# Cross-entropy loss on one core: a smoother taper of the fourteen loads, and twelve unread products ahead of the last ones

## The chip, the cores and the metric

The kernel runs on one core of one Trainium2 chip. The metric is device time in microseconds (us); a median over several runs is quoted, with the lowest and highest. The profile comes from one profiled execution, and its span (first to last instruction) is some 1.8 us shorter than the device time.

## The reference, cut to what matters

```python
def reference(logits, labels):            # logits [256, 32000] float32, labels [256] int32
    log_probs = logits - np.max(logits, axis=-1, keepdims=True)
    log_probs = log_probs - np.log(np.sum(np.exp(log_probs), axis=-1, keepdims=True))
    return np.array([-log_probs[i, labels[i]] for i in range(batch)])
```

The kernel leaves the maximum out: the loss of a row is log(sum of exp(x) times exp(-x at the label)). All 32.77 MB of logits must be read once.

## The kernel before

Two rows of the logits lie on each of 128 partitions, 64,000 columns in all, loaded in fourteen pieces. ScalarE takes the exp of each piece in place and accumulates its row sum. At the end VectorE adds the partial sums of the second row, TensorE multiplies them into a diagonal matrix that holds exp(-x at the label), a second product adds the sum of the last piece, ScalarE takes the log and one small transfer writes the result.

```python
CHUNKS = [
    14848, 12288, 8832, 6528, 4992, 3776, 2752,
    2368, 1856, 1344, 1344, 1152, 1024, 896,
]
...
        for i in range(2, len(CHUNKS) - 1):
            exps(i)
            if seen[0] == n_of[0] and i == HEAD - 1:
                ...                                   # row 0: reduce, product, log
        nc.vector.reduce_sum(out=sums[:, 1:2], in_=parts[1][:, :], axis=mybir.AxisListType.X)
        nc.tensor.matmul(lane[1][:, :], sums[:, 1:2], diag[1][:, :], start=True, stop=False)
        exps(len(CHUNKS) - 1)
        nc.tensor.matmul(lane[1][:, :], s_last[:, :], diag[1][:, :], start=False, stop=True)
        log_row(1)
        nc.sync.dma_start(...)                        # the 256 results
```

In what follows, "sums product" is the first of the two products at the end and "last product" the second. Each is float32 and appears as two passes of TensorE, a pair. A product whose passes run at TensorE's slow clock is called cold here, at its fast clock warm.

The softmax here doesn't subtract the row's maximum and nothing guards it: scores larger than these inputs give would overflow.

## Time and profile before

| | before |
|---|---|
| device time, median of 3 | 85.26 us (85.17 to 85.44) |
| span of the profiled run, whose device time was 85.8 | 84.0 us |
| bytes read, share of the load queue | 32.77 MB, 92.2% |
| ScalarE busy | 58.9 us, 70% |
| TensorE busy | 1.8 us |

The queue is busy nearly all the time, so the place to look is what comes after the last load has landed. The prediction shows the lines.

### The profile page before, as it was taken

To read this page: it belongs to the slowest core of one execution; us is meant where nothing else is said; L and a number is where in the kernel's file an instruction comes from. 1 tells how busy PE (TensorE), PEld (TensorE's weight loads), DVE (VectorE), ACT (ScalarE), POOL (GpSimd) and SP (SyncE) were. 2 spreads that over 40 slices of the span, in tenths; PEclk is the share of its full clock that TensorE was granted. 3 is DMA by queue.
4 is the path that set the end of the run, shared out by engine and by line. 5 is a ranking of instruction groups with operands and counts; after the bars stand their busy time and mean duration, and the time that the engine had idled before them with its cause. 6 is when DMAs were issued, how large, how long until landed. Compare 5 with 4: busy or idle time off the path is not lost.

```text
span 84.0 us, 126 instructions
## 1 busy us (share of the span) xinstructions
PE 1.8 (2%) x6; PEld 0.3 (0%) x6; DVE 0.8 (1%) x4; ACT 58.9 (70%) x34; POOL 3.0 (4%) x10
## 2 busy tenths in 40 slices
PE   0000000000000000000000002000000000000050
PEld 0000000000000000000000000000000000000000
DVE  0000000000000000000000200000000000000000
ACT  6000000001999998089999999999999999999960
POOL 3000000000072000000000000000000000000000
DMA  9787899998999989979989999999999999999300
GB/s 424 311 368 339 368 453 453 453 453 375 515 491 421 398 374 421 454 320 521 454 370 407 448 448 403 443 428 417 396 422 418 425 412 420 414 413 405 149 0 0
DMA packets 2226, 32.77 MB, mean 390 GB/s; under 512 B 433, under 2 KB 434, under 8 KB 1202
## 3 DMA queue, kind: packets, MB, share of 16 engines
q1 hardware_dynamic: 2018, 32.77, 92.2%
q10 hardware_dynamic: 144, 0.00, 0.1%
q0 software_dynamic: 64, 0.00, 0.1%
HBM read 32.77 MB, written 0.00 MB: 390 GB/s over the span
## 4 chain that ended last, share of the span: by engine, by line
DMA 74%; issue 13%; ACT 6%; SPq 2%; PE 1%
DMA x<-in_logits_dram 42%; DMA x_tail<-in_logits_dram 33%; ACT x_tail L112 6%; SPq L100 2%; PE lane L160 1%; ACT res L120 0%; ACT x L112 0%; ACT eg L148 0%
## 5 line engine op out<-in xcount | busy, mean ns | idle before, releaser
L112 ACT ACTIVATE x<-x 128x14848 f32<-128x14848 f32 (+5 forms) x6 | 40.7, 6790 | 21.2 <-DMA x<-in_logits_dram 21.2
L112 ACT ACTIVATE x_tail<-x_tail 128x1344 f32<-128x1344 f32 (+6 forms) x8 | 12.2, 1525 | 0.4 <-DMA x_tail<-in_logits_dram 0.4
L112 ACT ACTIVATE x_mid<-x_mid 128x3776 f32<-128x3776 f32 x1 | 3.3, 3349 | 0.0
L135 POOL DMA_INDIRECT g<-in_logits_dram,idx x2 | 2.1, 1036 | 0.6 <-issue 0.3
L91 ACT ACT_TABLE_LOAD x1 | 1.3, 1283 | 0.8 <-PEq L179 0.8
L155 PE MATMUL lane<-diag,sums 128*1 128x128 f32 x2 | 0.6, 396 | 51.0 <-DVE sums L154 51.0
L112 ACT ACTIVATION_READ_ACCUMULATOR x_tail<-x_tail 128x1 f32 x8 | 1.5, 186 | 0.0
L158 PE MATMUL lane<-diag,sums 128*1 128x128 f32 x2 | 0.6, 397 | 28.7 <-DVE sums L157 28.7
L112 ACT ACTIVATION_READ_ACCUMULATOR x<-x 128x1 f32 x6 | 1.1, 187 | 0.0
L120 ACT ACTIVATE res<-lane 1x128 f32<-1x128 f32 x2 | 0.5, 264 | 0.7 <-PE lane L160 0.7
L133 POOL TENSOR_TENSOR idx<-idx,lbl 128x2 int32<-128x2 int32 x1 | 0.2, 193 | 21.4 <-DMA lbl<-in_labels_dram 21.4
L150 DVE TENSOR_SCALAR diag<-ident,eg 128x128 f32<-128x128 f32 x2 | 0.5, 285 | 46.7 <-ACT eg L148 46.7
L160 PE MATMUL lane<-diag,s_last 128*1 128x128 f32 x2 | 0.6, 394 | 0.2 <-ACT x_tail L112 0.2
L157 DVE TENSOR_REDUCE sums<-parts 128x1 f32<-128x11 f32 x1 | 0.2, 164 | 29.1 <-ACT x_tail L112 29.1
masks.py:199 POOL TENSOR_SCALAR_AFFINE_SELECT ident<-ident 128x128 f32<-128x128 f32 x1 | 0.3, 292 | 0.1
L155 PEld LDWEIGHTS lane<-diag,sums 128*1 128x1 f32 x2 | 0.1, 80 | 51.0 <-DVE sums L154 51.0
masks.py:197 POOL MEMSET ident<- 128x128 f32 x1 | 0.2, 194 | 0.0
L154 DVE TENSOR_REDUCE sums<-parts 128x1 f32<-128x3 f32 x1 | 0.2, 156 | 3.7 <-ACT x L112 3.7
L148 ACT ACTIVATE eg<-g 128x2 f32<-128x2 f32 x1 | 0.2, 188 | 0.0
L112 ACT ACTIVATION_READ_ACCUMULATOR x_mid<-x_mid 128x1 f32 x1 | 0.2, 186 | 0.0
L158 PEld LDWEIGHTS lane<-diag,sums 128*1 128x1 f32 x2 | 0.1, 80 | 29.2 <-DVE sums L157 29.2
L131 POOL IOTA idx<- 128x2 int32 x1 | 0.1, 120 | 0.5 <-POOLq L179 0.5
(5 smaller groups left out, 0.5 us busy)
## 6 DMA issues: line engine op xcount, KB each, us to landing
x<-in_logits_dram SPq DMA_DIRECT2D x1, 7424.0 KB, 20.7
x<-in_logits_dram SPq DMA_DIRECT2D x1, 6144.0 KB, 35.1
x<-in_logits_dram SPq DMA_DIRECT2D x1, 4416.0 KB, 45.0
x<-in_logits_dram SPq DMA_DIRECT2D x1, 3264.0 KB, 51.8
x<-in_logits_dram SPq DMA_DIRECT2D x1, 2496.0 KB, 57.2
x_mid<-in_logits_dram SPq DMA_DIRECT2D x1, 1888.0 KB, 17.9
x_tail<-in_logits_dram SPq DMA_DIRECT2D x1, 1376.0 KB
x_tail<-in_logits_dram SPq DMA_DIRECT2D x2, 672.0 KB, 26.8
```

What stands on the lines that cost most here:

```text
L91: nc.scalar.preload_act_table_set("natural_log_exp_and_others")
L100: nc.sync.dma_start(out=t[:, a - base:b - base], in_=flat[:, a:b])
L112: nc.scalar.activation(out=t[:, a - base:b - base], in_=t[:, a - base:b - base], func=AF.Exp, accum_out=acc,)
L120: nc.scalar.activation(out=res[0:1, r:ROWS * P:ROWS], in_=lane[r][:, :], func=AF.Ln)
L133: nc.gpsimd.tensor_add(out=idx[:, :], in0=idx[:, :], in1=lbl[:, 0:2 * ROWS:2])
L135: nc.gpsimd.indirect_dma_start(out=g[:, r:r + 1], out_offset=None, in_=logits[:, :], in_offset=bass.IndirectOffsetOnAxis(ap=idx[:, r:r + 1 ...
L148: nc.scalar.activation(out=eg[:, :], in_=g[:, :], func=AF.Exp, scale=-1.0)
L150: nc.vector.tensor_scalar_mul(diag[r][:, :], ident[:, :], eg[:, r:r + 1])
L154: nc.vector.reduce_sum(out=sums[:, 0:1], in_=parts[0][:, :], axis=mybir.AxisListType.X)
L155: nc.tensor.matmul(lane[0][:, :], sums[:, 0:1], diag[0][:, :], start=True, stop=True)
L158: nc.tensor.matmul(lane[1][:, :], sums[:, 1:2], diag[1][:, :], start=True, stop=False)
L160: nc.tensor.matmul(lane[1][:, :], s_last[:, :], diag[1][:, :], start=False, stop=True)
```

## The change

It has two intents. First, the sizes of the loads fall more smoothly, to 576 columns instead of 896, so that less exp is left after the last landing. Second, TensorE is given twelve products that nobody reads shortly before the end, so that its last two products run at the array's fast clock. The row-0 log also moves one exp earlier on ScalarE (the row-0 product moves in the program as well), and the handling of the buffers is rewritten without changing which load waits for which.

```diff
 CHUNKS = [
-    14848, 12288, 8832, 6528, 4992, 3776, 2752,
-    2368, 1856, 1344, 1344, 1152, 1024, 896,
+    15872, 11840, 9216, 7104, 5056, 3904, 2944,
+    2176, 1536, 1280, 1024, 768, 704, 576,
 ]
+WARM_FROM = 7
+WARM = 12
...
+    warm = psum.tile([P, 512], F32, name="warm")
...
+            if i == WARM_FROM:
+                col = parts[1][:, seen[1] - 1:seen[1]]
+                for _ in range(WARM):
+                    nc.tensor.matmul(warm[0:1, 0:P], col, diag[0][:, :], start=True, stop=True)
```

## The prediction

> **What bounds the kernel now.** I read the page first: the DMA row of its second part, the queue part, then the chain that ended last. The last line here, from the queue part, is the rate over the whole span.
>
> ```profile
> DMA  9787899998999989979989999999999999999300
> ...
> q1 hardware_dynamic: 2018, 32.77, 92.2%
> ...
> HBM read 32.77 MB, written 0.00 MB: 390 GB/s over the span
> ...
> DMA 74%; issue 13%; ACT 6%; SPq 2%; PE 1%
> ```
>
> The logits pass through once, on one queue whose engines are busy from about 1 us to the 37th of 40 slices (2.1 us each). This change moves the same bytes in the same fourteen loads, and 2018 = 14 x 144 + 2 says one row packet for each of 128 partitions, 16 more per load, and two for the result. So the bulk cannot get shorter. What can is what comes after the last load lands; the timeline shows that end.
>
> ```profile
> 76.20 1.32 ACT L112 ACTIVATE x_tail<-x_tail 128x1344 f32<-128x1344 f32 x1 [0.18 <-DMA x_tail<-in_logits_dram]
> ...
> 77.63 1.16 ACT L112 ACTIVATE x_tail<-x_tail 128x1152 f32<-128x1152 f32 x1
> ...
> 78.91 1.06 ACT L112 ACTIVATE x_tail<-x_tail 128x1024 f32<-128x1024 f32 x1
> ...
> 79.98 0.95 ACT L112 ACTIVATE x_tail<-x_tail 128x896 f32<-128x896 f32 x1
> ...
> 80.31 0.59 PE L158 MATMUL lane<-diag,sums 128*1 128x128 f32 x2 [28.67 <-DVE sums L157]
> ...
> 81.07 0.58 PE L160 MATMUL lane<-diag,s_last 128*1 128x128 f32 x2 [0.18 <-ACT x_tail L112]
> 81.69 0.27 ACT L120 ACTIVATE res<-lane 1x128 f32<-1x128 f32 x1 [0.67 <-PE lane L160]
> 81.99 0.32 SPq L162 DMA_DIRECT2D out_dram<-res  x1
> ```
>
> The columns are start, duration, engine, line, operation and, in brackets, the idle time before it. Is the last exp, at 79.98, held by its data or by the exps ahead of it? The DMA view gives issue-to-landing for each load, here for the last one, and the timeline of the issuing queue gives its issue.
>
> ```profile
> 64.44 0.33 SPq L100 DMA_DIRECT2D x_tail<-in_logits_dram  x1
> ```
>
> ```profile
> x_tail<-in_logits_dram SPq DMA_DIRECT2D x1, 448.0 KB, 15.5
> ```
>
> 64.44 + 15.5 = 79.9: the data. The same sum for the others gives landings at 20.7, 35.9, 46.2, 53.9, 59.9, 64.4, (67.8), 70.5, 72.8, 74.5, 76.2, 77.6, 78.9 and 79.9; the one in brackets has no landing in the view and is interpolated. ScalarE starts almost every exp from 46 us on within 0.3 us of its landing: it keeps pace with the loads and has no backlog at the end. So the end is: last landing, one exp of 896 columns with its accumulate read, a 0.6 us product, a 0.27 us log, and some 2.3 us of output and finish to 84.0.
>
> **What the Trainium skill says.** "TensorE: Matmul & The Clock Gate", section "Single matmul latency", gives (219 + N)/1.2 ns cold and (398 + N)/2.4 warm. With N = 256, taking each of the two f32 passes over 128 columns as two cycles a column (my reading), cold is 396 ns; the group of the last product reads 394. So the trace agrees with a cold array, although it shows a granted clock of 1.00 throughout: that record does not show the gate, only durations will. The section "What you observe" of the same page puts the change to the fast clock some 4 us into sustained matmuls, within 0.5 us. No matmul of this trace is ever warm, so that is untested here. "ScalarE: Activation LUTs", section "What ACT_TABLE_LOAD costs", gives 186 ns + 0.833 N for an exp with immediates: 932 for 896 columns, measured 949; 12,554 for 14848, measured 12,576. It agrees. "DMA: Bandwidth & Descriptors", "Where 436 GB/s comes from", puts the fabric ceiling at 435 GB/s; the windows view has 411 in 70 to 78 us, so there is little rate left to win.
>
> **The change, part by part.**
>
> (1) Landings. Bytes, loads and row packets stay, so the last landing stays at 79.9. To place the others I fitted cost per column a and per load b: from 53.9 to 64.4, 8768 columns in two loads took 10.5 us; from 70.5 to 79.9, 7616 in six took 9.4. Solved, a = 1.18 ns and b = 0.07 us. Counting back from 79.9 through 576, 704, 768, 1024, 1280, 1536, 2176, 2944, 3904, 5056 and 7104 columns gives landings at 79.15 (704), 78.25, 77.3, 76.0, 74.4, 72.5, 69.9 (2944), 66.35, 61.7, 55.6 and 47.2 (9216). The first two come later than before: 15872 at 20.7 + 1024 x 1.24 ns = 22.0, and 27712 columns together at 35.9 + 576 x 1.18 ns = 36.6.
>
> (2) ScalarE against these landings. Start to start, a packed exp costs 0.833 N + 0.2 us (1024: 1.07), and about 0.3 in place of 0.2 where the next waits for its load (1152: 1.28). The second exp runs from 36.6 for 11840 columns, to 46.7, and the result of the gather about 0.1: ready at 46.8, but its next load lands at 47.2. So the order of issue to the slots stays safe (x_mid was issued at 46.50 and its successor is issued near 46.9, with 12160 columns of loads ahead of it, 14 us). From there: 4288 and 4928 columns end at 55.4, wait to 55.6; 7104 and the log of row 0, to 61.9; 5056 to 66.3; 3904 to 69.95; 2944 to 72.6 to 72.7; 2176 to 74.7; 1536 to 76.1; 1280 to 77.4; 1024 to 78.45; 768 to 79.3; 704 to 80.05. The last landing is 79.9, so a backlog of about 0.15 us is left. The last exp starts near 80.05, 0.07 later than before.
>
> (3) The last exp is 320 columns shorter: 320 x 0.833 = 0.27 us. With 0.07 lost ahead of it, its sum is ready 0.2 us earlier, at about 80.88 instead of 81.07.
>
> (4) Twelve products, two passes each. At 256 cycles a pass that is 24 x 213 ns = 5.1 us cold. They wait for the exp of 2176 columns, so they run from 74.8 to 79.9 at the slowest, before the sums product at about 80.4: they delay nothing. They leave through a PSUM tile that nobody reads. If the fast clock comes some 4 us in (near 78.8), it is there for the last two products. The last one then costs an estimated 109 + 273 = 0.38 us, from the page's section "Back-to-back issue gap" (N/2.4 + 2.5) and its latency formula, in place of 213 + 396 = 0.61: 0.23 less. I give it three chances in four: 5.1 us is not much above 4.
>
> (5) Moving the first row's product and log one exp earlier changes nothing at the end: both had long been done.
>
> Sum: 0.2 + 0.75 x 0.23 = 0.37, with the certain case 0.43. I take 0.4: 85.26 - 0.4 = 84.86, given as 84.85.
>
> **The rivals.**
> (a) ScalarE becomes the bound. From 46.5 us it idles only 0.4 us for data in all (the waits view), and the smoother taper gives less time per load: 704 columns take 0.83 us to load with b and 0.79 to compute. If landings come in a burst, or if the 0.3 us kind of start happens throughout, six short exps add 0.1 each, the start is 80.5, and the gain of (3) is gone; with the warm product the time is 85.2 or so, without it 85.4. For it: the margins in (2) are 0.1 to 0.25 us. Against it: packed starts are the normal kind once a backlog exists.
> (b) The array stays cold. Then only (3) is left: 85.05. A colder corner: the sums product occupies the array to about 80.83, and the last product starts at 80.88, so cold it nearly collides; a miss costs up to 0.1.
> (c) The shape of the loads changes the rate. The first rows are 63,488 bytes each and the last 2,304. A rate change of half a per cent is 0.4 us, as large as the whole effect. For it: b is small but real, and the engines do not end together (DMA share falls to 0.40 at 78.2 us, stragglers to 79.5). Against it: packets are equal in number. It would give 84.5 to 85.3.
>
> **Range and chances.** The three runs of before spread from 85.17 to 85.44, so noise is some 0.15. A gain of 0.4, with (a) and (b) taking up to 0.4 of it and (c) moving it 0.3 either way, gives 84.4 to 85.3. Two per cent would be 83.55 or 86.97. The end after the last landing is 4.1 us, and the change touches about half a microsecond of it; neither border is within reach unless the rate of the loads itself changes. Faster 0.01, same 0.98, slower 0.01.
>
> **What would show it right or wrong.** The last load should still land near 79.9 after the span's start; the last exp should take 0.68 us and start within 0.2 of that landing. The early warm products should read about 396 ns each and the late ones about 273, and the last product's pair should span 0.38 rather than 0.58. The last warm product must end before the sums product starts. A last exp that starts over 0.3 us after its landing makes (a) right; a last pair of 0.58 makes (b) right; a last landing off by more than 0.3 us makes (c) right, and then the number is wrong for a reason that the taper's sizes alone do not give.

## The result, and the profile after

| | before | after |
|---|---|---|
| device time, median | 85.26 us (85.17 to 85.44) | 84.95 us (84.95 to 84.96) |
| span of the profiled run | 84.0 us (device time 85.8) | 83.1 us (device time 84.96) |

The ratio is 0.9962, with a 95% interval of 0.9944 to 0.9979. Ratios here are the mean time of one kernel's runs over that of the other's of the same rounds, so they are not quite the ratio of the medians. The change is 0.31 us faster, clear of noise and well inside the 2% that counts as the same. The prediction was 84.85, in a range of 84.4 to 85.3.

From the page of the profile after, the load queue, the rate, the chain that ended last, and two of the groups (busy us and mean ns of one stand after the bar):

```profile
q1 hardware_dynamic: 2018, 32.77, 93.1%
...
HBM read 32.77 MB, written 0.00 MB: 394 GB/s over the span
...
DMA 55%; ACT 40%; PE 0%; SPq 0%; issue 0%; another core or an unknown queue 0%
...
L176 PE MATMUL warm<-diag,parts 128*1 128x128 f32 x24 | 5.1, 412 | 22.8 <-ACT x_tail L124 22.8
...
L180 PE MATMUL lane<-diag,s_last 128*1 128x128 f32 x2 | 0.4, 270 | 0.1
```

The same 2018 packets and 32.77 MB pass. The chain now runs through ScalarE for 40% of the span where it was 6%. That sounds like a new bound, but it is only that the exps now follow each other without a recorded wait; the experiment that takes an exp away tests it. The last product's passes take 270 ns where they took 394.

The end of the timeline after:

```profile
74.34 5.15 PE L176 MATMUL warm<-diag,parts 128*1 128x128 f32 x24 [22.77 <-ACT x_tail L124]
...
78.82 0.78 ACT L124 ACTIVATE x_tail<-x_tail 128x704 f32<-128x704 f32 x1
...
79.59 0.67 ACT L124 ACTIVATE x_tail<-x_tail 128x576 f32<-128x576 f32 x1
...
79.94 0.38 PE L178 MATMUL lane<-diag,sums 128*1 128x128 f32 x2 [0.45 <-DVE sums L177]
...
80.41 0.38 PE L180 MATMUL lane<-diag,s_last 128*1 128x128 f32 x2
80.82 0.27 ACT L132 ACTIVATE res<-lane 1x128 f32<-1x128 f32 x1 [0.47 <-PE lane L180]
81.12 0.32 SPq L182 DMA_DIRECT2D out_dram<-res  x1
```

The twelve products fill 74.34 to 79.49, clear of the sums product at 79.94. The last exp takes 0.67 us, the last pair 0.38. The last load was issued at 66.00 and landed 13.5 later, at 79.5:

```profile
66.00 0.33 SPq L112 DMA_DIRECT2D x_tail<-in_logits_dram  x1
```

```profile
x_tail<-in_logits_dram SPq DMA_DIRECT2D x1, 288.0 KB, 13.5
```

Set beside the trace of before (last landing at 79.9, output issued at 81.99), the end comes 0.87 us sooner, nearly three times what the clock shows. The rest is the late sample, as the first experiment shows.

### The profile page after: what moved, and what is told of

Read it like the earlier page. It is cut to its first block, busy times and chain, and to the rows that moved or that the text cites. A ratio compares the mean times of both kernels' runs of the same rounds, so it can differ in the third digit from the quotient of the medians.

```text
span 83.1 us, 174 instructions
## 1 busy us (share of the span) xinstructions
PE 6.5 (8%) x30; PEld 3.2 (4%) x30; DVE 0.8 (1%) x4; ACT 58.5 (70%) x34; POOL 3.0 (4%) x10
## 2 busy tenths in 40 slices
DMA packets 2226, 32.77 MB, mean 394 GB/s; under 512 B 433, under 2 KB 434, under 8 KB 1202
## 3 DMA queue, kind: packets, MB, share of 16 engines
q1 hardware_dynamic: 2018, 32.77, 93.1%
HBM read 32.77 MB, written 0.00 MB: 394 GB/s over the span
## 4 chain that ended last, share of the span: by engine, by line
DMA 55%; ACT 40%; PE 0%; SPq 0%; issue 0%; another core or an unknown queue 0%
DMA x<-in_logits_dram 55%; ACT x L124 27%; ACT x_tail L124 13%; ACT res L132 1%; PE lane L180 0%; SPq L112 0%
## 5 line engine op out<-in xcount | busy, mean ns | idle before, releaser
L124 ACT ACTIVATE x<-x 128x15872 f32<-128x15872 f32 (+6 forms) x7 | 45.5, 6506 | 21.3 <-DMA x<-in_logits_dram 21.3
L124 ACT ACTIVATE x_tail<-x_tail 128x2944 f32<-128x2944 f32 (+7 forms) x8 | 10.7, 1339 | 0.0
L176 PE MATMUL warm<-diag,parts 128*1 128x128 f32 x24 | 5.1, 412 | 22.8 <-ACT x_tail L124 22.8
L176 PEld LDWEIGHTS warm<-diag,parts 128*1 128x1 f32 x24 | 2.9, 124 | 25.1 <-ACT x_tail L124 23.3
```

The costliest lines, as they stand in the source:

```text
L124: nc.scalar.activation(out=t[:, a - base:b - base], in_=t[:, a - base:b - base], func=AF.Exp, accum_out=acc,)
L176: nc.tensor.matmul(warm[0:1, 0:P], col, diag[0][:, :], start=True, stop=True)
```

## The experiments

Kernels are compared only within the same rounds. "Below before" means medians.

### The kernel before, run again

Edit: none.

> The kernel before, unchanged, run as if it were a change. Its profiled run on record took 85.8 us against a median of 85.26, so the trace of before may be a late sample: in it the last load lands at 79.9, in the trace of after at 79.5. Theory A (the landings are the same and the old trace is a slow sample): a new profile of before has its span about 0.5 us shorter (83.5) and its last landing near 79.5. Rival B (the new sizes really bring the last load in 0.4 us earlier): the last landing of before is again at 79.8 to 80.0. Time 85.26 plus or minus 0.15 under both.

Measured: 85.28 us (85.14 to 85.61) against 85.29; the profiled run took 85.27, its span is 83.5. From its timeline:

```profile
63.90 0.33 SPq L100 DMA_DIRECT2D x_tail<-in_logits_dram  x1
...
79.44 0.95 ACT L112 ACTIVATE x_tail<-x_tail 128x896 f32<-128x896 f32 x1
...
80.54 0.59 PE L160 MATMUL lane<-diag,s_last 128*1 128x128 f32 x2 [0.20 <-ACT x_tail L112]
...
81.46 0.32 SPq L162 DMA_DIRECT2D out_dram<-res  x1
```

Its view of the transfers gives the same 15.5 us for the last load, so it landed at 63.90 + 15.5 = 79.4. Theory A holds and B falls: the loads of the changed kernel do not end earlier (79.5 against 79.4). In the old trace everything from the second exp on was late by one amount (35.94 against 35.36, and 79.98 against 79.44). From here on this trace stands for before. The difference at the end is then 81.46 - 81.12 = 0.34 us, which agrees with the clock: the last exp starts 0.15 later, takes 0.28 less, and the last pair takes 0.2 less. The kept traces hold the landings more exactly than the view: the last exp starts 0.02 after its landing here (79.42) and 0.12 after it in the changed kernel (79.48).

### The changed kernel again, as yardstick

Edit: none.

> The changed kernel unchanged, as the yardstick on this chip. 84.95 us, 0.30 below before; last exp starts within 0.15 us of its load's landing; last pair 0.38 us. Theory A above would put its last landing level with that of before_again.

Measured: 84.92 us (84.85 to 84.97), ratio 0.9953 (0.994 to 0.9966), 0.37 below before. The last exp starts at 79.60 and the last pair takes 0.38 us.

### The taper without the unread products

```diff
-WARM = 12
+WARM = 0
```

> The changed kernel with its twelve unread products taken out, nothing else. If the array warms only through them, the last product is cold again (pair 0.58 to 0.60 us instead of 0.38) and the time is 0.2 us above the changed kernel: 85.15, or 0.1 below before. The sums product ahead of it occupies a cold array to about 0.43 us after its start, and the last product may start up to 0.1 us later than its sum is ready. Rival: the warm products only look faster in the record and the time stays at 84.95.

Measured: 85.17 us (85.07 to 85.22), ratio 0.9981 (0.9968 to 0.9994), 0.12 below before. The end of its timeline:

```profile
79.68 0.67 ACT L124 ACTIVATE x_tail<-x_tail 128x576 f32<-128x576 f32 x1
...
80.03 0.58 PE L178 MATMUL lane<-diag,sums 128*1 128x128 f32 x2 [28.38 <-DVE sums L177]
...
80.49 0.58 PE L180 MATMUL lane<-diag,s_last 128*1 128x128 f32 x2
```

The pair is back at 0.58. The near collision that was feared between the two products costs nothing that shows: from the start of the last exp to that of the last product it is 0.81 us here (79.68 to 80.49) and 0.82 with warm products (79.59 to 80.41). So the products are worth about 0.25 us, and the taper alone about 0.12. This run keeps the moved log and the new handling of the buffers too; no run takes them away, but the steps of the changed kernel's trace (0.15 lost ahead of the last exp, 0.28 won in it) leave nothing of the 0.12 for them to explain.

### The unread products without the taper

```diff
+            if i == 8:
+                col = parts[1][:, seen[1] - 1:seen[1]]
+                for _ in range(12):
+                    nc.tensor.matmul(warm[0:1, 0:P], col, diag[0][:, :], start=True, stop=True)
```

in the kernel before, with its own PSUM tile.

> The kernel before with twelve unread products after its ninth load (1856 columns), the same place in time as in the changed kernel. If the two parts add up: last pair 0.38 us, time 0.2 below before, 85.05. If the warm products are worth nothing at the end of the chip's clock: 85.26.

Measured: 85.07 us (85.05 to 85.45), ratio 0.9982 (0.9967 to 0.9997), 0.22 below before; last pair 0.38 us.

```profile
80.56 0.38 PE L165 MATMUL lane<-diag,s_last 128*1 128x128 f32 x2 [0.40 <-ACT x_tail L113]
```

The parts add up: 0.12 + 0.22 = 0.34, against 0.31 and 0.37 for both together.

### The unread products too early

```diff
-WARM_FROM = 7
+WARM_FROM = 4
```

> The changed kernel with its twelve unread products moved ahead, from behind the exp of 2176 columns (at 74.3 us) to behind that of 5056 (at about 66), so that they end near 71 and the array is idle for some 9 us before the last two products. Theory (what counts is activity shortly before the end): the array is cold again at 80 us, last pair 0.58 us, time as without the products, 85.17. Rival (being used at all is enough, or it is the instruction fetch that the products warm): last pair 0.38, 84.92.

Measured: 85.14 us (85.09 to 85.24), ratio 0.9982, 0.16 below before. From the timeline of its TensorE and from its windows (the third number from the right is the granted clock, the share of its full speed that TensorE was given):

```profile
66.09 5.16 PE L176 MATMUL warm<-diag,parts 128*1 128x128 f32 x24 [14.55 <-ACT x L124]
...
80.36 0.59 PE L180 MATMUL lane<-diag,s_last 128*1 128x128 f32 x2
```

```profile
73.00:74.00 1.00, 0.00 (x0) 0.00 (x0) 0.00 (x0) 1.00 (x1) 0.00 (x0) 1.00 1.03 420
74.00:75.00 1.00, 0.00 (x0) 0.00 (x0) 0.00 (x0) 1.00 (x3) 0.00 (x0) 0.70 1.00 401
75.00:75.50 0.50, 0.00 (x0) 0.00 (x0) 0.00 (x0) 0.50 (x1) 0.00 (x0) 0.50 1.06 422
```

The same twelve products are worth nothing when 9 us of idleness follow: the pair is at 0.59 again. The record shows the clock falling to half. A mean of 0.70 in 74 to 75 us puts the step at 75 - 0.3/0.5 = 74.4, an estimated 3.2 us after the last unread product (66.09 + 5.16 = 71.25). So neither a count of products nor their instructions having been fetched explains the gain; recent activity does.

### Six, and eight, instead of twelve

```diff
-WARM = 12
+WARM = 6        # warm_half;  WARM = 8 in warm_eight
```

> The changed kernel with six unread products in place of twelve: 12 passes of 0.213 us, 2.6 us, from 74.3 to 76.9. In the three traces so far the fast clock came an estimated 2.7, 3.8 and 4.8 us into the products, worked out from how long the 24 passes took together (4.11, 4.64, 5.15 us). If the stretch of activity must be about that long, six are too few: last pair 0.58, time 85.17. If the switch only needs to be started and comes later by itself: 0.38 and 84.92. A mixture over the rounds is possible.

> The changed kernel with eight unread products: 16 passes of 0.213 us, 3.4 us of activity. Six left the last pair at 0.58 us in their profile and twelve were warm in every profile. If the stretch must fill a window of fixed places in time, eight give a mixture: some rounds near 84.92, some near 85.15. If a fixed length from the first product is needed (some 3 us), all are warm; the switch seen in the traces came an estimated 2.7 to 4.8 us in, so I expect the mixture, or mostly cold.

Measured with six: 85.09 us (85.04 to 85.6), ratio 0.9971, 0.21 below before, which lies between the cold kernels (0.12 and 0.16) and the warm ones, so the profile and not the median has to tell. The profiled run was its slowest, and cold:

```profile
74.82 2.72 PE L176 MATMUL warm<-diag,parts 128*1 128x128 f32 x12 [22.78 <-ACT x_tail L124]
...
80.87 0.58 PE L180 MATMUL lane<-diag,s_last 128*1 128x128 f32 x2
```

Measured with eight: 84.93 us (84.88 to 85.16), ratio 0.9965 (0.9948 to 0.9981), and warm in its profile:

```profile
74.32 3.57 PE L176 MATMUL warm<-diag,parts 128*1 128x128 f32 x16 [22.79 <-ACT x_tail L124]
...
80.37 0.38 PE L180 MATMUL lane<-diag,s_last 128*1 128x128 f32 x2
```

Between 2.7 and 3.6 us of activity lies the border, as far as one profile each can say. With eight, five of six runs lie from 84.88 to 85.00 and one is at 85.16, where a cold run would be; whether that one was cold is not known, since it has no profile (its clock is listed as 1.000, as in every run with six or no unread products, but also in two of the changed kernel's four). The pure mixture that I half expected did not show. Twelve cost nothing, because they end before the sums product, but they do not leave much margin. In two profiles all unread passes still ran at the slow pace and the last pairs were warm: with eight, and in the kernel with fifteen loads (further down), where 24 passes took 5.28 us and the fast clock came only in the 0.9 us before the sums product:

```profile
74.50 5.28 PE L176 MATMUL warm<-diag,parts 128*1 128x128 f32 x24 [22.26 <-ACT x_tail L124]
80.66 0.38 PE L178 MATMUL lane<-diag,sums 128*1 128x128 f32 x2 [0.89 <-DVE sums L177]
```

Nor does the fast clock last: wherever the passes show its coming, it went 3.4 us later by the record (79.2 to 82.6 in after, 71.0 to 74.4 with early products); only in the kernel before with unread products it lasted 6.8. In the run with one exp left out (below) it went at 81.53, 0.65 us after the last pair.

### Only the last load smaller

```diff
-    2368, 1856, 1344, 1344, 1152, 1024, 896,
+    2368, 1856, 1344, 1344, 1152, 1344, 576,
```

in the kernel before.

> The kernel before with the last two loads changed from 1024 and 896 columns to 1344 and 576, no other change. If only the size of the last exp counted: 0.27 below before, 85.02. By the sums of the prediction ScalarE is late: 1344 columns land 0.75 us before the last 576 and take 1.3, so the last exp starts about 0.55 later than in before (80.0 instead of 79.44) and ends 0.27 to 0.3 later: 85.55.

Measured: 85.66 us (85.44 to 85.75), ratio 1.0036 (1.0022 to 1.0049), 0.36 above before.

```profile
78.89 1.32 ACT L112 ACTIVATE x_tail<-x_tail 128x1344 f32<-128x1344 f32 x1 [0.41 <-DMA x_tail<-in_logits_dram]
...
80.21 0.67 ACT L112 ACTIVATE x_tail<-x_tail 128x576 f32<-128x576 f32 x1
```

The second-last load arrives late (ScalarE waits 0.41 us for it), and its exp holds up the last one until 80.21. A small last load alone makes the kernel slower: each load must be small enough beside its successor, and that is what the taper is for. To end at 576 in fourteen loads, the columns have to go to the front; in the changed kernel the first load has 15872.

### One exp left out

```diff
         for a, b, r in pieces[i]:
+            if i == 10:
+                nc.vector.memset(parts[r][:, seen[r]:seen[r] + 1], 0.0)
+                seen[r] += 1
+                continue
```

The result lacks 1024 columns of each second row: wrong.

> The changed kernel with the exp of its eleventh load (1024 columns) left out and a zero in place of its sum; the load itself stays. Wrong result on purpose. It takes 1.06 us of work from ScalarE shortly before the end. If the loads bind and ScalarE is only about 0.15 us behind, the last exp moves from 79.59 to about 79.45 and the time from 84.92 to about 84.78. If ScalarE is the bound and the landings in the view only follow its waits, the last exp moves up by more, to 79.0 or below, and the time to 84.3 or so.

Measured: 85.00 us (84.85 to 85.04), ratio 0.996 (0.9946 to 0.9973), 0.30 below before, so no better than the changed kernel.

```profile
78.02 0.84 ACT L128 ACTIVATE x_tail<-x_tail 128x768 f32<-128x768 f32 x1 [0.90 <-DMA x_tail<-in_logits_dram]
...
78.90 0.79 ACT L128 ACTIVATE x_tail<-x_tail 128x704 f32<-128x704 f32 x1
...
79.69 0.67 ACT L128 ACTIVATE x_tail<-x_tail 128x576 f32<-128x576 f32 x1
```

The exp of 1024 columns is gone, and ScalarE turns 0.90 us of the 1.06 into a wait for the next load. This run's earlier exps are 0.1 late (2944 columns at 69.65 against 69.54), so the exp of 768 starts, set against that, only 0.08 sooner, and the last one at most 0.02. The chain's 40% of ScalarE was therefore, as far as this test reaches, no bound ahead of the last exps: the loads are right behind it. I had expected 0.14 from this; the backlog ahead of these three exps is less than 0.1. The last exp gains least because of the exp just before it: by the landings in the kept trace of after the last two loads come 0.7 us apart (78.78 and 79.48), and the exp of 704 columns between them takes 0.78.

### Fifteen and thirteen loads

```diff
+    15872, 11840, 9216, 7104, 5056, 3776, 2752,                  # fifteen
+    2048, 1472, 1216, 960, 832, 704, 640, 512,
+    15872, 11840, 9216, 7488, 5312, 3904, 2880,                  # thirteen
+    2176, 1664, 1280, 1024, 768, 576,
```

> The changed kernel with one load more and a finer end: 3776, 2752, 2048, 1472, 1216, 960, 832, 704, 640, 512 in place of 3904, 2944, 2176, 1536, 1280, 1024, 768, 704, 576. The last exp is 64 columns shorter (0.05), one load more costs the fitted 0.07, so 0.02 above the changed kernel: 0.36 below before, no difference that five rounds can show. If the loads cost nothing each and ScalarE is never late, 0.05 below the changed kernel; if a load costs much more than 0.07 us, clearly above it.

> The changed kernel with one load less: 7488, 5312, 3904, 2880, 2176, 1664, 1280, 1024, 768, 576 in place of 7104, 5056, 3904, 2944, 2176, 1536, 1280, 1024, 768, 704, 576. The load saved is worth the fitted 0.07 us, but the steeper steps at the end leave ScalarE 0.1 us further behind; together 0.03 above the changed kernel, 0.35 below before. If ScalarE is not behind, 0.07 below the changed kernel.

Measured with fifteen: 85.34 us (85.19 to 85.83), ratio 0.9998 (0.9983 to 1.0014); with thirteen: 85.24 us (85.09 to 85.43), ratio 0.9999 (0.998 to 1.0017). Both expectations missed: each loses nearly all of the 0.37. In the profile of thirteen (one of its fastest runs, 85.10) the steeper steps keep ScalarE without a wait from 55.78 us on, and the last exp starts at 79.70, 0.1 behind the yardstick's 79.60; the other runs, up to 85.43, have no profile. The profile of fifteen fell on its slowest run:

> The kernel with fifteen loads once more, unchanged. Its first profile fell on its slowest run (85.83) and had the third load land at 47.5 in place of 46.9, though its first five loads are those of the changed kernel, so that profile cannot tell a late sample from a cost of the fifteenth load. Theory A (chance in the first loads): a typical profile has the third load at 46.9, the last exp at about 79.65, and the time near 84.95, 0.35 below before. Theory B (the fifteenth load costs more than the fitted 0.07 us): the time stays 0.2 to 0.4 above the changed kernel, near 85.25, and the third load may land at 46.9 all the same while the last exp starts at 79.8 or later.

Measured: 85.23 us (85.11 to 85.4), ratio 0.9994 (0.998 to 1.0008). Theory A falls: fifteen loads are slower by 0.3 to 0.4. But the profiled run, its fastest at 85.11, has the exp of the third load at 46.79 (46.89 in the yardstick) and the last one at 79.60, as the yardstick has, and issues its output at 81.07, 0.05 sooner. What is longer is the end: the wait of the issuing queue for the output to land, first of the yardstick, then of fifteen.

```profile
SPq L210 <- DMA out_dram<-res: 0.5, 1, 0.5
```

```profile
SPq L210 <- DMA out_dram<-res: 0.7, 1, 0.7
```

It is 0.7 in both profiles of fifteen, and 0.5 in the twelve other profiles. But the output itself is not slower: in the kept traces it lands 1.12 to 1.13 us after its issue in all fourteen. At its end the program checks the semaphores of its transfers (the counters that tell of a landing) in a fixed order, one check after the other. With fourteen loads the output has the semaphore that is checked last, so that the other checks are done while it is under way, and the queue goes on 0.08 us after the landing. With fifteen it has the one that is checked second, the other checks follow the landing, and the queue goes on after 0.31; with thirteen, last but one, after 0.14. This 0.22 more, less the 0.05, is the whole 0.18 by which the span of fifteen is longer than the yardstick's. Why the unprofiled runs lose more, and scatter, stays open. No version here beats the changed kernel.

## Why the prediction was right

**The bound.** Right. With the same bytes and packets the last landing stayed: 79.5 against 79.4 in the trace of before that is no late sample. The prediction counted from 79.9 in the late trace, so all its clock times are about 0.4 late; most of its differences are not touched. Its own test for the third rival ("a last landing off by more than 0.3 us") would have given a false alarm for that reason: it compared one trace with a late one.

**Landings (1).** Right in spacing. Landings of after, from the issues and the view of the transfers, are at 36.1 and 46.9 for the second and third load and 77.9, 78.7 and 79.5 for the last three; predicted were 36.6, 47.2, 78.25, 79.15 and 79.9. The spacings of the last three are 0.8 and 0.8 against 0.9 and 0.75.

**ScalarE against the landings (2).** The mechanism was right, the term was mis-sized. The last exp was to start 0.07 us later than in before; it starts 0.15 later (79.59 and 79.60 against 79.44). The landings to the hundredth separate it: the last load lands 0.06 later, and the exp waits 0.12 behind its landing instead of 0.02. The backlog of 0.15 that was predicted is thus 0.12, made mostly by the exp of 704 columns; the 0.07 came out too small in part because 64.44 + 15.5 = 79.94 was taken as 79.9. Two more slips changed nothing: the 0.83 us that 704 columns take to load is without b (0.90 with it), and output and finish take 2.0 us from the end of the log, not 2.3. The 0.3 in place of 0.2 for a start that waits is no cost of its own: in before the exp of 1024 columns starts 0.02 after its load has landed (78.907 against 78.884), so the 0.1 more is the wait itself.

**The shorter exp (3).** Right: 0.27 predicted, 0.95 - 0.67 = 0.28 measured. With the later start, 0.13 is left instead of 0.2, and the taper alone measured 0.12.

**The products (4).** Right. Predicted 5.1 us for twelve, ended before the sums product: 5.15 us, from 74.34 to 79.49. Passes of about 273 ns instead of 396: 270 instead of 394. The pair: 0.38 instead of 0.58. The saving is 0.20 in the traces and 0.22 on the clock, where 0.23 had been put. All eight profiles with twelve, or with eight, shortly before the end were warm, so three chances in four look careful; but there was some luck in it. The doubt that 5.1 us is not much above 4 was sound: with fifteen loads the fast clock came after the 24th pass.

**The row-0 log (5).** Not tested apart; the steps of the sum leave nothing for it.

**The sum.** 0.43 for the certain case, 0.4 taken; the steps in the traces give -0.15 + 0.28 + 0.20 = 0.33, and the clock 0.31 and 0.37.

**The rivals.** ScalarE as the bound: not in the changed kernel, but the run with only the last load smaller shows such a case, 0.36 us slower. A cold array: it came with six products and with twelve early ones. A changed rate of the loads: not seen in the changed kernel. With thirteen, fourteen and fifteen loads the last one landed at 79.43, 79.48 and 79.48, in one profile each, so the 0.07 us a load of the fit does not show there; what one more load cost was found elsewhere.

## What to carry to other kernels

In a kernel bound by its loads, look first at what follows the last landing, and shrink the loads towards the end so that each exp is done before its successor has landed; a small last load alone makes it worse. Where the end hangs on one or two float32 products and TensorE was idle before, a few unread products that end shortly ahead of them are worth 0.2 us here, provided that they last some 3.5 us and end shortly before their use: 0.3 to 2 us ahead of the sums product was right in eight profiles, 9 us was too early, and nothing between was tried. Before explaining a difference of traces, compare each profiled run's time with its kernel's median: here one late sample would have tripled the effect.

## What the Trainium skill lacked or had wrong

- "TensorE: Matmul & The Clock Gate", section "What you observe", puts the fast clock some 4 us into sustained matmuls, within 0.5. Worked out from the time that the 24 passes took (5.15, 4.64 and 4.11 us), it came an estimated 2.7 to 4.8 us in, and in the first profile of fifteen loads, where all 24 were slow (5.28), later still, but before 6.2 (80.66 - 74.50): a wider spread. 2.7 us of products (six) left the last pair cold and 3.6 us (eight) did not, in one profile each.
- The same page, section "Single matmul latency", has no float32 case. Taking each of the two passes over 128 columns as 256 cycles gives 396 ns cold and 273 warm; measured 394 and 270.
- The same page does not say how the record of the granted clock reads before its first change. Here the view gives 1.00: the trace of before has 1.00 throughout with cold passes of 394 ns, and so have all five traces without a warm pass. 0.50 shows in the nine traces with fast passes alone, after them: from 74.4 us in the kernel with early products, from 82.6 in after.
- "ScalarE: Activation LUTs", section "What ACT_TABLE_LOAD costs", says that back-to-back activations overlap by 93 ns. It does not say what reading the accumulator adds: here the read takes 186 ns and overlaps by about 0.1 us with the exp before it and with the exp after it, so that packed exps follow each other after 0.833 ns a column and 0.2 us (1024 columns: 1.05 in after, 76.94 to 77.99).
- No page gives the cost of one more load on a queue that is already full. The fit says 0.07 us, the last landing did not move between fourteen and fifteen loads (79.48), and the kernel with fifteen was 0.3 to 0.4 us slower, 0.2 of it because its output's semaphore is checked second and not last.
